# A rebuilt guess for the order of instructions, inverse roots on VectorE, and attention in smaller pieces

## The chip, the cores and the metric

The kernel runs on one core of one Trainium2 chip. The time is that of one execution on the device in microseconds; the figure for the kernel before is the median of three runs, 856.73 us (855.6 to 857.45). Engines go by the profile's names: PE is TensorE's matmuls, PEld its loads of weights, DVE is VectorE, ACT ScalarE, POOL GpSimd, and SP the queue from which the DMAs are issued.

## The reference

A trunk of two layers over 256 tokens of 2048 features. Cut to what matters:

```python
def hybrid_layer(x, c, cos, sin, layer_idx, ...):
    mod = (c @ w_ada + b_ada)[:, None, :]                  # adaLN: 2048 x 6144, one row
    shift, scale, gate = jnp.split(mod, 3, axis=-1)
    h = rms_norm(x, g_pre) * (1 + scale) + shift
    z = h @ w_in                                           # 2048 x 6144
    u, g_pool, q, k, v, g_diff = jnp.split(z, splits, axis=-1)
    pool_out = multiscale_pool(u, w_pool, pool_scale) * jax.nn.silu(g_pool)
    q, k = apply_rope(q, cos, sin), apply_rope(k, cos, sin)
    att = diff_attention(q, k, v, lam)                     # softmax(map 0) - lam * softmax(map 1), chunk-causal
    att = rms_norm(att, subln_g) * (1.0 - lam_init)        # per head of 128
    diff_out = att * jax.nn.silu(g_diff)
    y = jnp.concatenate([pool_out, diff_out], axis=-1) @ w_out   # 2048 x 2048
    return x + (1 + gate) * rms_norm(y, g_post)
```

## The kernel before

**Units.** The weights of the two projections come as tiles `raw` of 128 x 1024 float32 (512 KB). Each is split into a high and a low half that TensorE takes (`whi`, a cast on ACT; `wlo`, a subtraction on DVE), and so are the left operands (`hhi`, `hlo`). A product is hi x hi + hi x lo + lo x hi. One `raw` is one *unit* of twelve matmuls of 128 x 512 into two accumulators `acc`. A layer has 96 units of the input projection (12 blocks of 512 columns, 8 pairs of row tiles each) and 32 of the output projection. The text numbers units and raws through both layers from 0: layer 0 has 0 to 95 and 96 to 127, layer 1 128 to 223 and 224 to 255. "Slot 225" is the place in PE's order where 225 units are done. The ring of `raw` has four buffers, those of `whi` and `wlo` three, PSUM four banks for `acc` and four for the rest (`ps`).

**AdaLN.** The row `mod` is no matmul. A tile `ada` of 512 KB (ring of three) is loaded, and one DVE instruction multiplies it by the broadcast `c` and sums along the row (method `ada`): 184 such products beside eight at the start. Each column's pair of products ends with three small steps into `A` and `B`, which `make_h` needs. The last third of a layer gives its gate `G`.

**Side work.** Beside the units run generators, each a chain of pieces: `make_h` (normalized operands), `rope`, `pool_group` (trailing means as products with `band`, then `ps<-hf,Gw`, `z<-ps,cols,z` and the parts `hhi`, `hlo`), and `heads` for a pair of heads: scores (`ps<-z,z`), maxima `nm`, exponentials `t` on ACT, 1/sum `rs`, combined maps, their transposes (`ps<-consts,t`), copies `aT` on ACT, value products (`ps<-z,aT`), squares `ass`, inverse root, scaled product `z<-ps,af,z`, and `make_cat`, which transposes the result (`ps<-consts,z`) and splits it. Units of the output projection need these parts (`cat`), four of pool groups and four of pairs of heads.

**Order.** All engines run in program order (`tc.manual_schedule()`), and the program decides it while it is written. `Watched` (L70) passes each instruction to `Clock.note` (L103), which keeps a guess of each engine's time, so in the profile every instruction bears the line L86. After each unit, `advance` (L679) lets those side pieces run whose inputs are due by the guess within `SLACK` of TensorE's guessed time and for which PSUM banks are free. Then `beside` (L757) takes the `ada` products that have been dealt to the unit: while VectorE's guessed time is not ahead of TensorE's, and in any case until no more than `TODO` = 1 is left over.

**Inverse roots.** `rsqrt` (L282) serves the pre-norm of layer 0 (`xr`, two columns) and every pair of heads (`ar`, four columns): GpSimd forms x, DVE a guess from the bits of x in two steps, GpSimd three Newton rounds of four steps; `heads` then multiplies by `r2` there. `rms` (L304) does the other norms (`ya`, `yb`, `xa`, `xb`) on DVE, one column each.

## Time and profile before

| | before |
|---|---|
| median of three runs | 856.73 us |
| profiled execution | 856.63 us |
| its span | 854.8 us |
| granted clock over the span | 0.986 |
| VectorE | 899 rows of its order, 695.5 us busy (81%) |
| ScalarE | 543.5 us busy (64%) |
| GpSimd | 45.8 us busy (5%), 129 instructions |
| DMA | 245.08 MB, mean 287 GB/s |

The page's table of 40 slices shows where the layers lie: a slice is 21.4 us, a digit the busy tenths in it, and PEclk the granted clock.

```profile
PE   3899899999999999998979999999999999889995
DVE  6789898888898977988786788888789989667665
POOL 2000000000000001142000000000000000030400
PEclk9999999999999999999989999999999999999998
DMA  9899999999898975688925999999998888443742
```

Slices 15 to 18 are layer 0's attention, 20 and 21 the turn-over to layer 1, 34 to 37 layer 1's attention; POOL's digits stand where the inverse roots are.

### The profile page before, as it was taken

What the parts mean: (1) busy time and instruction counts of PE and PEld (TensorE: products, weight loads), DVE (VectorE), ACT (ScalarE), POOL (GpSimd) and SP (SyncE); (2) the same over time, 40 slices, a digit from 0 to 9 for tenths busy, and PEclk for the clock granted to TensorE, in tenths of its full rate; (3) what the DMA queues carried; (4) which work ended last, traced back from release to release, by engine and by line L of the source; (5) the groups of instructions that cost most, each with busy time, mean ns of one, the idle gap of its engine ahead of it and who ended that gap; (6) DMA issues with size and microseconds to landing.
All of it is one profiled execution on the core that took longest, in us unless ns stands there. A gap on an engine that the chain in (4) does not pass through costs nothing.

```text
span 854.8 us, 11938 instructions
## 1 busy us (share of the span) xinstructions
PE 803.6 (94%) x4058; PEld 667.5 (78%) x4058; DVE 695.5 (81%) x1194; ACT 543.5 (64%) x950; POOL 45.8 (5%) x129
## 2 busy tenths in 40 slices
PE   3899899999999999998979999999999999889995
PEld 1678688889888887786758888888889898677884
DVE  6789898888898977988786788888789989667665
ACT  4688787766556666664655656776665567666561
POOL 2000000000000001142000000000000000030400
PEclk9999999999999999999989999999999999999998
DMA  9899999999898975688925999999998888443742
GB/s 340 287 396 327 330 370 344 370 367 350 304 355 325 331 251 166 207 287 292 324 73 182 343 365 383 326 346 322 357 326 333 309 320 265 130 148 109 261 148 99
DMA packets 68239, 245.08 MB, mean 287 GB/s; under 512 B 7729, under 2 KB 8017, under 8 KB 67665
## 3 DMA queue, kind: packets, MB, share of 16 engines
q1 hardware_dynamic: 67890, 244.14, 80.3%
q8 instruction: 32, 0.52, 0.3%
q10 hardware_dynamic: 288, 0.17, 0.1%
q14 instruction: 29, 0.24, 0.1%
HBM read 242.17 MB, written 2.11 MB: 286 GB/s over the span
## 4 chain that ended last, share of the span: by engine, by line
PE 75%; DVE 10%; ACT 5%; DMA 4%; POOL 3%; issue 2%; SPq 0%; DVEq 0%; ACTq 0%
PE acc L86 69%; PE ps L86 6%; DVE wlo L86 3%; ACT whi L86 2%; POOL arh L86 2%; DVE ada L86 2%; DMA raw<-in_w_out 1%; ACT t L86 1%; DMA z<-in_w_ada 1%; DVE z L86 1%; DMA ada<-in_w_ada 1%; DVE rt L86 1%; DMA raw<-in_w_in 1%; DVE x L86 1%; ACT sqj L86 1%
## 5 line engine op out<-in xcount | busy, mean ns | idle before, releaser
L86 ACT CAST whi<-raw 128x1024 fp32r<-128x1024 f32 x247 | 259.4, 1053 | 205.1 <-PE acc L86 182.7
L86 DVE TENSOR_TENSOR wlo<-raw,whi 128x1024 fp32r<-128x1024 f32 x247 | 301.3, 1223 | 81.2 <-ACT whi L86 80.7
L86 PE MATMUL acc<-whi,hhi 128*128 128x512 f32 x860 | 344.3, 400 | 6.0 <-ACT hhi L86 2.5
L86 PE MATMUL acc<-whi,hlo 128*128 128x512 f32 x860 | 337.8, 393 | 1.3 <-DVE hlo L86 1.3
L86 PE MATMUL acc<-wlo,hhi 128*128 128x512 f32 x860 | 337.8, 393 | 0.7 <-DVE wlo L86 0.7
L86 DVE SCALAR_TENSOR_TENSOR ada<-ada,cb 128x1024 f32<-128x1024 f32 x184 | 223.7, 1219 | 5.2 <-DMA ada<-in_w_ada 4.8
L86 PEld LDWEIGHTS acc<-whi,hhi 128*128 128x128 f32 x860 | 163.0, 190 | 45.0 <-ACT acc L86 4.4
L86 PEld LDWEIGHTS acc<-whi,hlo 128*128 128x128 f32 x860 | 162.7, 189 | 37.3 <-DVE hlo L86 2.6
L86 PEld LDWEIGHTS acc<-wlo,hhi 128*128 128x128 f32 x860 | 163.1, 190 | 33.8 <-DVE wlo L86 2.1
L86 ACT ACTIVATE z<-acc 128x512 f32<-128x512 f32 x164 | 88.5, 591 | 1.5 <-PE acc L86 1.5
L86 ACT COPY acc<-z 128x512 f32<-128x512 f32 x123 | 68.7, 585 | 3.1 <-DVE rt L86 3.1
L86 PE MATMUL acc<-hhi,whi 128*128 128x256 f32 x256 | 43.1, 288 | 3.1 <-ACT whi L86 2.0
L86 ACT ACTIVATE t<-ps,nm 128x128 f32<-128x128 f32 x64 | 26.0, 420 | 30.9 <-DVE nm L86 30.9
L86 POOL TENSOR_SCALAR arx<-ass 128x4 f32<-128x4 f32 x8 | 4.1, 517 | 728.6 <-ACT sqj L86 728.3
L86 PE MATMUL acc<-hlo,whi 128*128 128x256 f32 x256 | 41.7, 286 | 0.2 <-DVE hlo L86 0.2
L86 PE MATMUL acc<-hhi,wlo 128*128 128x256 f32 x256 | 41.6, 285 | 0.0
L86 PEld LDWEIGHTS acc<-hhi,whi 128*128 128x128 f32 x256 | 36.6, 193 | 5.4 <-ACT whi L86 2.4
L86 PEld LDWEIGHTS acc<-hlo,whi 128*128 128x128 f32 x256 | 35.7, 194 | 0.4 <-DVE hlo L86 0.4
L86 PEld LDWEIGHTS acc<-hhi,wlo 128*128 128x128 f32 x256 | 35.7, 194 | 0.0
L86 PE MATMUL ps<-consts,t 128*128 128x128 f32 x112 | 17.2, 284 | 17.6 <-issue 12.4
L86 PEld LDWEIGHTS ps<-consts,t 128*128 128x128 f32 x112 | 14.0, 147 | 22.0 <-issue 14.1
L86 PE MATMUL ps<-z,z 64*128 64x128 f32 (+1 forms) x128 | 19.1, 371 | 8.3 <-ACT t L86 7.5
(144 smaller groups left out, 596.8 us busy)
## 6 DMA issues: line engine op xcount, KB each, us to landing
raw<-in_w_in SPq DMA_DIRECT2D x192, 512.0 KB, 5.7
ada<-in_w_ada SPq DMA_DIRECT2D x184, 512.0 KB, 5.7
raw<-in_w_out SPq DMA_DIRECT2D x64, 512.0 KB, 4.6
z<-in_w_ada SPq DMA_DIRECT2D x8, 512.0 KB, 11.4
x<-in_x SPq DMA_DIRECT2D x2, 1024.0 KB, 7.6
Gw<-in_w_pool SPq DMA_DIRECT2D x8, 256.0 KB, 6.4
Gw<-gate SPq DMA_DIRECT2D x2, 1024.0 KB, 4.9
out<-x SPq DMA_DIRECT2D x8, 256.0 KB, 2.7
```

What stands on the lines that cost most here:

```text
L86: return f(*args, **kw)
```

## The change

Four things are done at once.

- `Clock` is rebuilt. It knows the operation of each instruction and has costs per engine (fixed, per element, for an accumulator, and until the result is seen), a price for a change of ScalarE's table, a DMA link with its rate, regions of a tile in place of whole tiles, the rings of buffers, and a TensorE that is slow for a while after a pause.
- `TODO` = (8, 1), with a method `put_off`: up to eight `ada` products may be left over, unless they are the own layer's shift or scale, when it is one; towards a layer's end the number falls with the units that are left, to none in the last five.
- `rsqrt` runs on VectorE, from x/2, with the guess in one step and each round in three (two for one column). It yields after every step, the multiplication by `r2` joins its last round, and `rms` uses it. GpSimd has no work left.
- In `heads` the copies `aT` are a step of their own, the value products a later one, and the inverse root begins a piece later. The pre-norm is one piece at the third lead product.

The matmuls, casts and loads are the same in number and shape, and `ORDERS`, `RATE`, `EARLY` and `SLACK`, which shape the plan, are unchanged. VectorE has 976 rows in place of 899.

```diff
@@ -91,34 +92,97 @@
-    FIXED = {"tensor": 0.0, "vector": 0.07, "scalar": 0.09, "gpsimd": 0.15, "sync": 0.0}
-    EACH = {"tensor": 0.42e-3, "vector": 1.04e-3, "scalar": 0.85e-3, "gpsimd": 2.3e-3, "sync": 1.43e-3}
+    COST = {"vector": (0.07, 1.05e-3, 0.01, 0.13), "scalar": (0.085, 0.86e-3, 0.13, 0.15), "gpsimd": (0.25, 2.3e-3, 0.0, 0.15)}
+    TABLES = ((AF.Exp, 1), (AF.Silu, 2), (AF.Sin, 3))
+    MB_US, LANDING = 0.40, 1.6
+    COLD = (2.0, 3.4)
+    RINGS = {"raw": 4, "ada": 3, "whi": 3, "wlo": 3, "acc": 4}
...
-    def note(self, key, outs, ins):
+    def note(self, key, op, outs, ins, total, table):
+        size = lambda x: math.prod(x.shape[1:])
+        outs, ins = ([x for x in xs if not x.tensor.name.startswith(("in_", "out_"))] for xs in (outs, ins))
+        t = was = self.now[key]
         for x in ins:
-            t = max(t, self.wrote.get(x.tensor.name, 0.0))
+            t = max(t, self.latest(self.wrote, x))
+            if key != "tensor" and x.tensor.name.startswith(("acc", "ps")):
+                t = max(t, self.latest(self.used, x))
         for x in outs:
-            if key != "tensor":
-                t = max(t, self.used.get(x.tensor.name, 0.0))
-        t += self.FIXED[key] + n * self.EACH[key]
-        self.now[key] = t
-        done = t + (1.5 if key == "sync" else 0.15)
+            if key != "tensor" or not self.wrote.get(x.tensor.name):
+                t = max(t, self.latest(self.used, x))
+        if "dma" in op:
+            self.now[key] = t + 0.35
+            x = (outs + ins)[0]
+            self.link = max(self.link, t + 0.8) + size(x) * x.shape[0] * 4e-6 / self.MB_US
+            end, done = t, self.link + self.LANDING
+        elif key == "tensor":
+            n, dt, began = size(outs[0]), ins[-1].dtype, t
+            if op == "transpose":
+                t += 0.109
+            elif dt == F32:
+                t += max(0.109, 0.835e-3 * n) * (1 if ins[0].shape[0] == DQK else 2)
+            else:
+                t += 0.0135 + 0.4167e-3 * n if dt == F32R else 0.08
+
+            if began - was > self.COLD[0]:
+                self.cold = began + self.COLD[1]
+            t = max(t, min(self.cold, 2 * t - began))
+            end, done = t, t + 0.27
+            self.now[key] = t
+        else:
+            fixed, each, accum, after = self.COST[key]
+            if table and table[0] != self.table:
+                self.table = table[0]
+                t += 1.29
+            t += fixed + each * max(size(x) for x in outs + ins) + total * accum
+            end, done = t, t + after
+            self.now[key] = t
         for x in ins:
-            self.used[x.tensor.name] = max(self.used.get(x.tensor.name, 0.0), t)
+            self.mark(self.used, x, end)
         for x in outs:
-            self.wrote[x.tensor.name] = self.used[x.tensor.name] = done
+            self.mark(self.wrote, x, done)
+            self.mark(self.used, x, done)
         self.last = max(self.last, done)
 
...
-    def rsqrt(self, ss, n, mul, tag):
-
-        gp = self.nc.gpsimd
+    def rsqrt(self, ss, n, mul, tag, end=None):
+
+
+        v = self.nc.vector
...
-        gp.tensor_scalar(x, ss, mul, EPS, op0=ALU.mult, op1=ALU.add)
+
+        v.tensor_scalar(x, ss, 0.5 * mul, 0.5 * EPS, op0=ALU.mult, op1=ALU.add)
         yield y
-        self.guess(yi, x)
-        for _ in range(3):
-            gp.tensor_tensor(h, y, y, op=ALU.mult)
-            gp.tensor_tensor(h, h, x, op=ALU.mult)
-            gp.tensor_scalar(h, h, -0.5, 1.5, op0=ALU.mult, op1=ALU.add)
-            gp.tensor_tensor(y, y, h, op=ALU.mult)
+        v.tensor_scalar(yi, x.bitcast(I32), -0.5, 0x5F3759DF - (1 << 22) - (1 << 31), op0=ALU.mult, op1=ALU.add)
         yield y
-
-    def guess(self, yi, x):
-
-        v = self.nc.vector
-        v.tensor_scalar(yi, x.bitcast(I32), 1, None, op0=ALU.logical_shift_right)
-        v.tensor_scalar(yi, yi, -1, 0x5F3759DF, op0=ALU.mult, op1=ALU.add)
+        for i in range(3):
+            v.scalar_tensor_tensor(h, y, x, y, op0=ALU.mult, op1=ALU.mult) if n == 1 else v.tensor_tensor(h, y, y, op=ALU.mult)
+            yield y
+            if n > 1:
+                v.tensor_tensor(h, h, x, op=ALU.mult)
+                yield y
+            if i == 2 and end is not None:
+                v.tensor_tensor(y, y, end, op=ALU.mult)
+            v.scalar_tensor_tensor(y, h, 1.5, y, op0=ALU.subtract, op1=ALU.mult)
+            yield y
...
     def rms(self, parts, tag):
+        s1 = self.t(self.sp, [P, 1], tag + "s")
+        self.nc.vector.tensor_reduce(s1, parts, axis=AX.X, op=ALU.add)
+        yield s1
+        yield from self.rsqrt(s1, 1, 1.0 / D, tag)
...
     def pre_norm(self):
-        for r in self.rsqrt(s1, NST, 1.0 / D, "xr"):
-            self.xr = [r[:, st : st + 1] for st in range(NST)]
-            yield
+        (r,) = self.together(self.rsqrt(s1, NST, 1.0 / D, "xr"))
+        self.xr = [r[:, st : st + 1] for st in range(NST)]
...
-    TODO = 1
+    TODO = (8, 1)
...
             if i == 2:
-                next(norm, None)
+                self.pre_norm()
...
     def beside(self, u):
         self.advance()
         self.todo += u.extras
-        while self.todo and (self.nc.now["vector"] <= self.nc.now["tensor"] + self.AHEAD or len(self.todo) > self.TODO):
+        while self.todo and (self.nc.now["vector"] <= self.nc.now["tensor"] + self.AHEAD or len(self.todo) > self.put_off()):
             self.ada(*self.todo.pop(0))
+
+    def put_off(self):
+
+        l, nt, _ = self.todo[0]
+        left = sum(u.l == self.l for u in self.units[self.at :])
+        return min(self.TODO[l == self.l and nt < 32], left - 5)
...
         yield 0
+        while self.turned_a:
+            yield 0
+        self.turned_a = True
+        aT = [self.t(self.pp, [P, 3, P], "aT") for _ in range(2)]
+        for h in range(2):
+            nc.scalar.copy(aT[h].rearrange("p i q -> p (i q)"), bt[h][:, 0 : 3 * P])
+        self.live -= 2
+        yield 1
+        self.turned_a = False
         av = self.ps()
         for h in range(2):
-            aT = self.t(self.pp, [P, 3, P], "aT")
-            nc.scalar.copy(aT.rearrange("p i q -> p (i q)"), bt[h][:, 0 : 3 * P])
-            self.live -= 1
             hs = slice((h0 + h) * P, (h0 + h + 1) * P)
...
         yield 0
...
-        (yf,) = self.together(self.rsqrt(ss, 4, 1.0 / P, "ar"))
-        f = sm("af", 4)
-        gp.tensor_tensor(f, yf, r2[:, :, 0], op=ALU.mult)
         yield 0
-        yield 0
+
```

Where instructions move, at three places. The first is VectorE in layer 0, from the `wlo` of raw 100 on; unit 99 needs the `hlo` of the last pool group, which is the second `hlo` here. Before:

```order
L86 SCALAR_TENSOR_TENSOR ada_2921,mod_166<-ada_2921,cb_92 128x1024
L86 SCALAR_TENSOR_TENSOR ada_2949,mod_166<-ada_2949,cb_92 128x1024
L86 SCALAR_TENSOR_TENSOR z_378<-ps_3166,cols_98,z_378 128x256 x2
L86 TENSOR_TENSOR hlo_3190<-z_378,hhi_3189 128x512
L86 TENSOR_TENSOR wlo_3199<-raw_2955,whi_3198 128x1024
L86 SCALAR_TENSOR_TENSOR z_378<-ps_3193,cols_98,z_378 128x256 x2
L86 TENSOR_TENSOR hlo_3238<-z_378,hhi_3237 128x512
L86 SCALAR_TENSOR_TENSOR ada_3069,mod_166<-ada_3069,cb_92 128x1024
L86 TENSOR_TENSOR wlo_3245<-raw_3017,whi_3244 128x1024
```

After the change (`nm`, RECIPROCAL, `co` and `t` belong to one pair of heads; `co` and three rows of `t` are left out):

```order
L87 SCALAR_TENSOR_TENSOR z_377<-ps_3162,cols_98,z_377 128x256 x2
L87 TENSOR_TENSOR hlo_3180<-z_377,hhi_3179 128x512
L87 TENSOR_TENSOR wlo_3184<-raw_2948,whi_3183 128x1024
L87 SCALAR_TENSOR_TENSOR ada_2942,mod_166<-ada_2942,cb_92 128x1024
L87 SCALAR_TENSOR_TENSOR ada_3007,mod_166<-ada_3007,cb_92 128x1024
L87 SCALAR_TENSOR_TENSOR ada_3065,mod_166<-ada_3065,cb_92 128x1024
L87 TENSOR_REDUCE nm_2955<-ps_3205 128x1 x2
L87 TENSOR_REDUCE nm_2955<-ps_3206 128x1 x2
L87 RECIPROCAL rs_2957<-s_2956 128x8
...
L87 SCALAR_TENSOR_TENSOR t_3235<-t_3235,co_3245 128x256
L87 SCALAR_TENSOR_TENSOR z_377<-ps_3213,cols_98,z_377 128x256 x2
L87 TENSOR_TENSOR hlo_3254<-z_377,hhi_3253 128x512
```

The last pool group's `z` and `hlo` stood right behind raw 100's `wlo`; now three products and one pair's softmax stand between.

The second place is VectorE in layer 0's output projection, from the `wlo` of raw 119 to that of raw 123. Before:

```order
L86 TENSOR_TENSOR wlo_3947<-raw_3880,whi_3946 128x1024
L86 TENSOR_TENSOR z_3953<-raw_3886,z_3952 128x1024
L86 TENSOR_TENSOR z_3958<-acc_3522,Gw_3409 128x512
L86 TENSOR_TENSOR z_3958<-acc_3523,Gw_3409 128x512
L86 SCALAR_TENSOR_TENSOR ada_3871,mod_167<-ada_3871,cb_92 128x1024
L86 TENSOR_TENSOR wlo_3979<-raw_3908,whi_3978 128x1024
L86 TENSOR_TENSOR wlo_3997<-raw_3929,whi_3996 128x1024
L86 TENSOR_TENSOR wlo_4015<-raw_3950,whi_4014 128x1024
```

After the change:

```order
L87 TENSOR_TENSOR wlo_3896<-raw_3826,whi_3895 128x1024
L87 TENSOR_TENSOR z_3902<-raw_3832,z_3901 128x1024
L87 TENSOR_TENSOR z_3907<-acc_3497,Gw_3379 128x512
L87 TENSOR_TENSOR z_3907<-acc_3498,Gw_3379 128x512
L87 SCALAR_TENSOR_TENSOR ada_3851,mod_167<-ada_3851,cb_92 128x1024
...
L87 SCALAR_TENSOR_TENSOR ada_3890,mod_167<-ada_3890,cb_92 128x1024
L87 TENSOR_TENSOR wlo_3934<-raw_3857,whi_3933 128x1024
L87 SCALAR_TENSOR_TENSOR ada_3893,mod_167<-ada_3893,cb_92 128x1024
L87 TENSOR_TENSOR wlo_3955<-raw_3875,whi_3954 128x1024
L87 SCALAR_TENSOR_TENSOR ada_3925,mod_167<-ada_3925,cb_92 128x1024
L87 TENSOR_TENSOR wlo_3976<-raw_3899,whi_3975 128x1024
```

The one product between the raws has become four, with the rows of `A` and `B` of a column left out here.

The third is VectorE in layer 1's attention, from the `wlo` of raw 227 on; each pair of heads has `nm`, RECIPROCAL, `co` and four `t`, of which the rows at the ends are shown. Before:

```order
L86 TENSOR_TENSOR wlo_7061<-raw_6875,whi_7060 128x1024
L86 TENSOR_REDUCE nm_6952<-ps_7034 128x1 x2
L86 RECIPROCAL rs_6954<-s_6953 128x8
...
L86 SCALAR_TENSOR_TENSOR t_7079<-t_7079,co_7089 128x256
L86 TENSOR_REDUCE nm_6955<-ps_7052 128x1 x2
L86 RECIPROCAL rs_6957<-s_6956 128x8
...
L86 SCALAR_TENSOR_TENSOR t_7096<-t_7096,co_7106 128x256
L86 TENSOR_TENSOR wlo_7113<-raw_6910,whi_7112 128x1024
L86 TENSOR_TENSOR wlo_7139<-raw_6948,whi_7138 128x1024
```

After the change:

```order
L87 TENSOR_TENSOR wlo_7009<-raw_6834,whi_7008 128x1024
L87 TENSOR_TENSOR wlo_7043<-raw_6873,whi_7042 128x1024
L87 TENSOR_REDUCE nm_6916<-ps_7026 128x1 x2
L87 RECIPROCAL rs_6918<-s_6917 128x8
...
L87 SCALAR_TENSOR_TENSOR t_7061<-t_7061,co_7071 128x256
L87 TENSOR_REDUCE nm_6919<-ps_7034 128x1 x2
L87 RECIPROCAL rs_6921<-s_6920 128x8
...
L87 SCALAR_TENSOR_TENSOR t_7078<-t_7078,co_7088 128x256
L87 TENSOR_TENSOR wlo_7095<-raw_6912,whi_7094 128x1024
L87 TENSOR_TENSOR wlo_7113<-raw_6972,whi_7112 128x1024
```

The two chains stood behind raw 227's `wlo` and ahead of raw 228's; now raw 228's `wlo` stands ahead of them and raw 229's behind. On PE the scores that these chains take stood at slot 225 and stand at slot 226.

## The prediction

> **What bounds the kernel now.** I read the page's shares and its chain first, then the waits of PE, then PE's timeline at each wait.

> ```profile
> span 854.8 us, 11938 instructions
> PE 803.6 (94%) x4058; PEld 667.5 (78%) x4058; DVE 695.5 (81%) x1194; ACT 543.5 (64%) x950; POOL 45.8 (5%) x129
> PE 75%; DVE 10%; ACT 5%; DMA 4%; POOL 3%; issue 2%; SPq 0%; DVEq 0%; ACTq 0%
> ```

> TensorE is busy in 94% of the span, and three quarters of the chain are its matmuls, which the change leaves alone in number and shape. A different order can therefore only win or lose part of the 854.8 - 803.6 = 51.2 us in which PE stands still, and what the throttle takes beside that. Here is what PE waited for (us in total, times, the longest):

> ```profile
> PE ps L86 <- issue: 12.4, 1, 12.4
> PE ps L86 <- ACT t L86: 7.5, 7, 2.0
> PE ps L86 <- DVE t L86: 5.3, 1, 5.3
> PE acc L86 <- DVE hlo L86: 1.5, 2, 1.3
> ```

> The 12.4 us are the start and the 5.3 us the turn-over between the layers; both hang on chains that the change barely touches. What can move are the waits of attention: 7.5 us behind ScalarE's exponentials (`t`), and single ones behind the left operands of the output projection. PE's timeline gives them one by one (start, duration, work, idle before it and who ended that):

> ```profile
> 357.48 0.70 PE L86 MATMUL ps<-z,z 64*128 64x128 f32 x5 [1.04 <-ACT t L86]
> 365.98 0.70 PE L86 MATMUL ps<-z,z 64*128 64x128 f32 x5 [0.78 <-ACT aT L86]
> 391.61 1.10 PE L86 MATMUL ps<-consts,z 128*128 128x128 f32 x4 [1.07 <-DVE z L86]
> 399.97 0.50 PE L86 MATMUL acc<-whi,hlo 128*128 128x512 f32 x1 [1.30 <-DVE hlo L86]
> 735.27 0.48 PE L86 MATMUL ps<-z,z 64*128 64x128 f32 x2 [1.51 <-ACT t L86]
> 736.07 0.70 PE L86 MATMUL ps<-z,z 64*128 64x128 f32 x5 [0.32 <-ACT t L86]
> 737.68 0.85 PE L86 MATMUL ps<-z,z 64*128 64x128 f32 x5 [0.32 <-ACT t L86]
> 761.25 0.49 PE L86 MATMUL ps<-z,z 64*128 64x128 f32 x2 [1.99 <-ACT t L86]
> 762.06 1.65 PE L86 MATMUL ps<-z,z 64*128 64x128 f32 x6 [0.32 <-ACT t L86]
> ```

> Layer 0's attention costs 1.04 + 0.78 + 1.07 + 1.30 = 4.2 us, layer 1's 2.15 us at 735 to 738 and 2.31 us at 761 to 762. The second pair costs more than its idle time. The table of stretches (busy time of PE, PEld, DVE, ACT, POOL, then granted clock, DMA share, GB/s) has:

> ```profile
> 340.00:400.00 60.00, 55.63 (x293) 44.51 (x292) 51.77 (x114) 35.62 (x92) 19.45 (x49) 1.00 0.73 252
> 400.00:430.00 30.00, 29.47 (x127) 23.56 (x128) 23.59 (x30) 17.99 (x28) 0.00 (x0) 1.00 0.91 320
> 733.00:742.00 9.00, 6.85 (x32) 4.64 (x31) 3.80 (x11) 7.10 (x26) 0.00 (x0) 0.81 0.39 117
> 760.00:770.00 10.00, 8.43 (x34) 6.52 (x35) 5.27 (x13) 5.42 (x18) 3.32 (x12) 0.83 0.18 52
> ```

> After the two waits of layer 1 the clock dropped: 9.00 x 0.19 and 10.00 x 0.17 are 1.7 us each. Layer 1's waits thus cost 2.15 + 1.7 + 2.31 + 1.7 = 7.9 us. This is the largest prize in reach.

> **The inverse root on VectorE.** Before, GpSimd did 13 small steps for a pair of heads, with two of VectorE's in between:

> ```profile
> L86 POOL TENSOR_TENSOR arh<-ary 128x4 f32<-128x4 f32 x24 | 11.2, 466 | 7.3 <-DVE ary L86 6.0
> DVE ary L86 <- POOL arx L86: 8.3, 4, 3.7
> 433.43 0.16 DVE L86 SCALAR_TENSOR_TENSOR yay<-yah,yay 128x1 f32<-128x1 f32 x1
> 433.62 0.22 DVE L86 SCALAR_TENSOR_TENSOR yah<-yay,yau 128x1 f32<-128x1 f32 x1
> 391.20 1.12 DVE L86 SCALAR_TENSOR_TENSOR z<-ps,af,z 128x128 f32<-128x128 f32 x4 [1.76 <-POOL af L86]
> 21.55 0.62 DVE L86 TENSOR_SCALAR t<-x,xry 128x256 f32<-128x256 f32 x2 [2.01 <-POOL xry L86]
> ```

> VectorE now issues 12 such steps for a pair where it issued 2. Its dependent small steps start 433.62 - 433.43 = 0.19 us apart, so a pair costs it 10 x 0.19 = 1.9 us more, the eight pairs 15 us. In exchange VectorE no longer stands 8.3 us before the guess or 1.76 us before the scaled product. In layer 0 the four chains add 7.6 us to 340 to 400, where VectorE has 60.00 - 51.77 = 8.2 us idle: it fits, though only just. The ends are -3.7 us (its longest wait for GpSimd, were all of that PE's) and +7.6 us (were none covered); I take nothing for the chain itself and let its delay count where the order below puts it on PE's path. The pre-norm's wait of 2.01 us turns into 11 dependent steps of about 0.19 us: 2.1 us of VectorE in its place, so 0 at the start (ends -0.5 and +0.5). The turn-over's and the last norm's chains lose two steps each, 0.4 us in three chains of layer 0's turn-over together and 0.2 us at the end.

> **Layer 0, unit 99.** This is the first place where the new order bears on PE. Unit 99 multiplies by the last pool group's parts, whose `z` and `hlo` stand on VectorE now behind three adaLN products (`ada`) and one pair's maxima and softmax steps.

> ```profile
> 335.42 1.22 DVE L86 SCALAR_TENSOR_TENSOR ada<-ada,cb 128x1024 f32<-128x1024 f32 x1
> 336.56 1.22 DVE L86 TENSOR_TENSOR wlo<-raw,whi 128x1024 fp32r<-128x1024 f32 x1
> 739.73 1.14 DVE L86 TENSOR_REDUCE nm<-ps 128x1 f32<-128x128 f32 x4
> 748.29 2.35 DVE L86 TENSOR_TENSOR wlo<-raw,whi 128x1024 fp32r<-128x1024 f32 x2
> 333.20 0.87 DVE L86 SCALAR_TENSOR_TENSOR z<-ps,cols,z 128x256 f32<-128x256 f32 x2
> 334.81 0.69 DVE L86 TENSOR_TENSOR hlo<-z,hhi 128x512 fp32r<-128x512 f32 x1 [0.74 <-ACT hhi L86]
> 334.25 1.50 PE L86 MATMUL ps<-z,aT 128*128 128x128 f32 x12
> ```

> ```profile
> 722.00 0.39 PE L86 MATMUL acc<-wlo,hhi 128*128 128x512 f32 x1
> 722.23 0.39 PE L86 MATMUL acc<-whi,hlo 128*128 128x512 f32 x1
> ```

> A unit is twelve matmuls that start 0.23 us apart, about 2.73 us. A product occupies VectorE for 336.56 - 335.42 = 1.14 us; maxima, exponentials and softmax steps take (748.29 - 739.73) / 2 = 4.28 us. Unit 100's `wlo` goes ahead of them and ends, by my walk along the new order, at about 332.7. Then 332.7 + 3 x 1.14 + 4.28 = 340.4, the two `z` 0.87, and ScalarE's `hhi` about 0.7: 342.0. PE came to this slot at 334.25 and has its small products to do there; one score product, the pool's product and the value products are in the slot now, which brings it to about 338.0. It waits 4.0 us. As 2.15 us in three pieces dropped the clock at 735, I charge 1.7 us too. In exchange the 4.2 us of before's four waits find their inputs ready, because VectorE does while PE stands what it did in them. Sum: 4.0 + 1.7 - 4.2 = **+1.5 us** (ends: -4.2 if the group is on time, +5.7 if no later wait goes).

> [...]

> **Layer 0's output projection.** Now up to eight products may be put off, and they come due before the layer ends. By the order, seven of them are still owed at the `wlo` of raw 119 and one at that of raw 127.

> ```profile
> 399.84 1.21 DVE L86 TENSOR_TENSOR wlo<-raw,whi 128x1024 fp32r<-128x1024 f32 x1
> 424.72 1.23 DVE L86 TENSOR_TENSOR wlo<-raw,whi 128x1024 fp32r<-128x1024 f32 x1 [2.57 <-ACT whi L86]
> ```

> That is 6 x 1.14 = 6.8 us more for VectorE, against 30.00 - 23.59 = 6.4 us idle in 400 to 430: +0.4 us if all its idle time served, +3.0 us if the last 2.57 us come too late. I take +1.0, and -0.4 for the shorter norms: **+0.6 us**. The cover is thin: each product more would cost PE its 1.14 us.

> **Layer 1's attention.** The second pair's scores go one unit later (slot 226, not 225), when ScalarE has freed their banks, so of the 2.15 + 1.7 us some 0.6 stay. But VectorE's two chains of 4.28 us now stand ahead of raw 229's `wlo`. They begin after raw 228's, near 740.9, and end at 749.5; the `wlo` is there at 750.7. PE ends unit 224 at 733.8 (735.27 - 1.51), does unit 225 by 736.5, scores and 0.6 us of waiting by 738.5, units 226 to 228 by 746.7 and a group of transposes by 747.2; so it waits 3.4 us for unit 229, with 1.7 us of clock behind it. The wait at 761 goes whole. With 1.5 us more for the last pairs' operands (a walk along the order, ends 0 and 3.5) the stage loses 0.6 + 3.4 + 1.7 + 1.5 = 7.2 us against 7.9: **-0.7 us** (ends -5.8 if 229 is on time, +1.3).

> **The rest.** In early layer 0 some pieces change places around units 10 to 20. PE's waits there are among these:

> ```profile
> PE acc L86 <- ACT acc L86: 2.4, 2, 1.9
> PE acc L86 <- ACT z L86: 1.2, 1, 1.2
> ```

> By the order the 1.2 us grow somewhat and the 1.9 us shrink: +0.3 us (ends -1 and +1), an estimate. In layer 1 the late products have slack by my walk: the last of them ends near 800 and the gate is used after 815. The other pieces hide behind matmuls. Sum: 0 + 0.3 + 1.5 + 0.6 - 0.7 - 0.2 = +1.5 us on the profiled execution's 856.63 us, which stands 0.1 us below the median of 856.73: **858.1 us**. About 0.2%, 1.7 us, is what a measurement of this kernel tells from no change, so "same" is 855.0 to 858.4.

> **The rivals.** *The waits go and nothing takes their place* (0.30). VectorE idles 8.2 us in 340 to 400, and ScalarE more; if the softmax steps run ahead of my walk by a unit (2.7 us), units 99 and 229 wait 1 us or so without the clock. Then layer 1 gives -5.1 in place of -0.7, layer 0 about -1 in place of +1.5: 858.1 - 4.4 - 2.5 = 851.2, and 853 where one of the two holds; I write 852 (850 to 855). Against it: both chains are strictly serial on VectorE in the order's rows.

> *The products put off saturate the output projection of layer 0* (0.20). DMA stands at a share of 0.91 in 400 to 430 at 320 GB/s. A raw or `ada` tile is 512 KB:

> ```profile
> ada<-in_w_ada SPq DMA_DIRECT2D x184, 512.0 KB, 5.7
> ```

> Between raws 119 and 131 twelve raws and eleven `ada` tiles of 0.52 MB fall due where it was four: 12 MB in 12 x 2.73 = 33 us, 365 GB/s, against 320 / 0.91 = 352 at a full share. That is 1.2 us late by bandwidth alone; if VectorE also has no cover, the group before the turn-over starts 1.2 + 3.0 + 1.0 us later than I charged: 863 us (861 to 865). It decides from the point where more than five products are owed at raw 119; the order says seven. Against it: DMA had slack before 400, and raws fetched early there lighten the rest.

> *The order turns out not to matter* (0.08): PE's waits shift but keep their sum, as ring depths and not program order set them; 856.6.

> **How the numbers follow.** The forecast has 0.42 and by itself a range of 855.5 to 861; half of it lies within 0.2%, half slower. Faster: 0.30 + 0.01 = 0.31. Same: 0.21 + 0.06 = 0.27. Slower: 0.21 + 0.20 + 0.01 = 0.42. A tenth is left out below 851, in the first rival, and somewhat under a tenth above 863.5.

> **What would show it.** Right: POOL's busy time near zero and VectorE's up by some 14 us; no PE wait at 735 to 738 and at 761; one of 3 to 5 us before a product with the fourth pool group's `hhi` near 340, with the clock down behind it; one of 3 us behind `wlo` near 748; waits of 0.5 to 1 us behind `wlo` at 412 to 425, DMA share there above 0.95. Wrong: if those at 340 and 748 are missing the first rival holds; if the turn-over begins 5 us later than 430, the second.

## The result, and the profile after

| | before | after |
|---|---|---|
| median (lowest to highest) | 856.78 us (855.6 to 857.45) | 870.02 us (868.26 to 870.63) |
| ratio, 95% interval | 1 | 1.0153 (1.0134 to 1.0171) |
| profiled execution, its span | 856.63 us, 854.8 us | 870.22 us, 868.4 us |

Two executions among the experiments below, one of 1626 us (b3) and one of 1349 us (e2), are left out of their medians and ratios.

The changed kernel is 1.5% slower. The forecast of 858.1 us said slower by about a tenth of this, and the range, up to 863.5 us, missed it too. The head of the page after, with the shares of the chain and the rows of the 40 slices for VectorE, GpSimd and the granted clock:

```profile
span 868.4 us, 11915 instructions
PE 808.9 (93%) x4058; PEld 671.6 (77%) x4058; DVE 708.4 (82%) x1271; ACT 543.5 (63%) x950; POOL 0.2 (0%) x4
DVE  7788899888888966789986788788888979667765
POOL 0000000000000000000000000000000000000000
PEclk9999999999999998999979999999999999999998
PE 68%; DVE 16%; DMA 6%; ACT 5%; issue 4%; SPq 0%; DVEq 0%; ACTq 0%
```

GpSimd is empty and VectorE has 12.9 us more, as forecast. PE's idle time grew from 51.2 to 868.4 - 808.9 = 59.5 us, and its busy time by 5.3 us with the same matmuls. Of that 868.4 x 0.019 - 854.8 x 0.014 = 4.5 us is clock, which fell from 0.986 to 0.981 over the span. In the chain 7% of the span went from PE to VectorE (10% to 16%) and DMA (4% to 6%). What PE waited for after the change (us in total, times, longest):

```profile
PE acc L87 <- ACT hhi L87: 6.6, 6, 2.5
PE acc L87 <- DVE wlo L87: 5.1, 4, 2.4
PE acc L87 <- ACT acc L87: 3.3, 5, 1.0
PE ps L87 <- ACT t L87: 3.1, 3, 2.1
PE acc L87 <- DVE hlo L87: 2.1, 1, 2.1
```

The waits behind the exponentials `t` fell from 7.5 to 3.1 us, which the change was able to do; in their place PE waits for operands of the big products, `hhi`, `wlo` and `hlo` (3.1, 0.7 and 1.5 us before). PE's timeline after, at the waits that the text uses:

```profile
344.51 0.59 PE L87 MATMUL acc<-whi,hhi 128*128 128x512 f32 x1 [2.45 <-ACT hhi L87]
416.81 0.80 PE L87 MATMUL acc<-wlo,hhi 128*128 128x512 f32 x1 [2.37 <-DVE wlo L87]
759.19 0.49 PE L87 MATMUL acc<-whi,hhi 128*128 128x512 f32 x1 [1.14 <-ACT whi L87]
761.33 0.79 PE L87 MATMUL acc<-wlo,hhi 128*128 128x512 f32 x1 [1.65 <-DVE wlo L87]
800.37 1.60 PE L87 MATMUL ps<-z,aT 128*128 128x128 f32 x12 [1.01 <-DVE hlo L87]
815.39 1.01 PE L87 MATMUL ps<-consts,z 128*128 128x128 f32 x4 [0.53 <-DVE z L87]
819.00 0.63 PE L87 MATMUL acc<-whi,hlo 128*128 128x512 f32 x1 [2.12 <-DVE hlo L87]
```

To see where the 13.6 us of span arise, the two traces are laid beside each other by units: for each unit the start of its first matmul after, less that before. The growth of this difference over a stretch of units is what the stretch lost.

| units | lost | forecast |
|---|---|---|
| start to 95 | +0.7 | +0.3 |
| 95 to 116 (layer 0's attention) | +2.8 | +1.5 |
| 116 to 127 (layer 0's output projection) | +4.5 | +1.0 |
| 127 to 219 (turn-over, layer 1's input projection) | +1.0 | -0.4 |
| 219 to 238 (layer 1's attention) | -1.9 | -2.2 |
| 238 to 243 (last operands) | +6.7 | +1.5 |
| 243 to the end | -0.2 | -0.2 |

Two rows hold most of the miss: 3.5 us in layer 0's output projection and 5.2 us at layer 1's last operands. Of the second, about 1.3 us is a group of value products (804.57 to 805.82) that stood ahead of unit 238 before and changed rows; units 219 to 243 together lost 4.8 us, where the forecast had -0.7. The first, as stretches of whole units (116 to 125; busy time of PE, PEld, DVE, ACT, POOL, then clock, DMA share, GB/s). Before:

```profile
402.38:428.12 25.74, 25.21 (x110) 20.04 (x108) 19.33 (x25) 16.14 (x24) 0.00 (x0) 1.00 0.94 332
```

After:

```profile
405.90:436.20 30.30, 26.84 (x110) 21.12 (x109) 28.90 (x46) 15.45 (x23) 0.00 (x0) 0.94 0.97 351
```

VectorE went from 19.33 to 28.90 us: eleven products where there were three, 8 x 1.14 = 9.1 us. It stood idle for 6.4 us of the stretch before; after, it is busy in 95% of it. Of PE's 4.6 us more, 2.9 are idle time and 1.6 are busy time at the lower clock (0.94) that follows the wait of 2.37 us. DMA is nearly full as well (a share of 0.97).

### The profile page after: what moved, and what is told of

Read it like the earlier page. It is cut to its first block, busy times and chain, and to the rows that moved or that the text cites. A ratio compares the mean times of both kernels' runs of the same rounds, so it can differ in the third digit from the quotient of the medians.

```text
span 868.4 us, 11915 instructions
## 1 busy us (share of the span) xinstructions
PE 808.9 (93%) x4058; PEld 671.6 (77%) x4058; DVE 708.4 (82%) x1271; ACT 543.5 (63%) x950; POOL 0.2 (0%) x4
## 4 chain that ended last, share of the span: by engine, by line
PE 68%; DVE 16%; DMA 6%; ACT 5%; issue 4%; SPq 0%; DVEq 0%; ACTq 0%
PE acc L87 63%; DVE wlo L87 5%; PE ps L87 5%; DMA ada<-in_w_ada 4%; DVE ada L87 3%; DVE z L87 2%; ACT whi L87 2%; DMA raw<-in_w_in 1%; DMA z<-in_w_ada 1%; DVE rt L87 1%; ACT t L87 1%; DVE t L87 1%; ACT z L87 1%; ACT hhi L87 1%; DVE arh L87 0%
## 5 line engine op out<-in xcount | busy, mean ns | idle before, releaser
L87 DVE TENSOR_TENSOR wlo<-raw,whi 128x1024 fp32r<-128x1024 f32 x247 | 300.2, 1222 | 81.7 <-ACT whi L87 81.0
L87 PE MATMUL acc<-whi,hhi 128*128 128x512 f32 x860 | 346.2, 403 | 12.4 <-ACT hhi L87 6.0
L87 PE MATMUL acc<-z,hhi 128*128 128x512 f32 x72 | 22.3, 391 | 0.6 <-ACT acc L87 0.6
L87 DVE TENSOR_TENSOR hlo<-hf,hhi 128x512 fp32r<-128x512 f32 (+1 forms) x15 | 9.8, 656 | 14.3 <-ACT hhi L87 13.1
## 6 DMA issues: line engine op xcount, KB each, us to landing
raw<-in_w_in SPq DMA_DIRECT2D x192, 512.0 KB, 5.6
ada<-in_w_ada SPq DMA_DIRECT2D x184, 512.0 KB, 6.0
raw<-in_w_out SPq DMA_DIRECT2D x64, 512.0 KB, 4.3
z<-in_w_ada SPq DMA_DIRECT2D x8, 512.0 KB, 11.4
```

Of the source, the lines that this page charges most:

```text
L87: return f(*args, **kw)
```

## The experiments

Each run is set beside the kernel before on the same chip; the ratio carries the 95% interval, and two runs are compared by their ratios, since they can come from different chips. The columns on the right are the loss by stretches of units as above, from the one profiled execution of each run. Single executions scatter: b3 and e2, which have the same order up to unit 95, begin it 3 us apart. So a row's first column and its sum are good to some 3 us, a stretch further on to about 1.

| run | median us | ratio (95%) | to 116 | 116-127 | 127-219 | 219-243 |
|---|---|---|---|---|---|---|
| the change | 870.0 | 1.0153 (1.0134-1.0171) | +3.5 | +4.5 | +1.0 | +4.8 |
| a5_no_debt | 871.3 | 1.0171 (1.0143-1.0199) | +13.6 | -0.5 | -0.3 | +4.8 |
| a3_old_clock | 859.8 | 1.0054 (1.0035-1.0073) | +7.2 | -1.3 | -0.6 | -3.1 |
| a2_gp_roots | 867.5 | 1.0135 (1.0114-1.0155) | +8.0 | -1.2 | -0.5 | +3.4 |
| a4_before_roots | 861.9 | 1.0070 (1.0045-1.0094) | +8.8 | -1.2 | -0.2 | -0.9 |
| b3_roots_same_order | 860.5 | 1.0050 (1.0030-1.0069) | +1.0 | -0.5 | -0.2 | +1.5 |
| b1_clock_only | 863.6 | 1.0074 (1.0045-1.0102) | +4.0 | -1.2 | +1.5 | +3.8 |
| b2_pieces | 867.7 | 1.0123 (1.0107-1.0138) | +12.4 | -1.2 | +0.2 | -0.5 |
| b4_roots_double | 876.7 | 1.0226 (1.0210-1.0243) | +11.6 | -0.4 | -0.2 | +7.1 |
| g1_one_round | 862.1 | 1.0045 (1.0028-1.0061) | +3.8 | +3.4 | +0.1 | -1.9 |
| a6_hold99 | 872.5 | 1.0181 (1.0156-1.0206) | +8.1 | +4.0 | +0.7 | +4.5 |
| c4_pool98 | 872.3 | 1.0183 (1.0159-1.0207) | +9.0 | +2.2 | +0.6 | +4.6 |
| c1_slack4 | 887.5 | 1.0364 (1.0331-1.0396) | +10.9 | +4.7 | +7.1 | +6.1 |
| c3_tail | 871.7 | 1.0172 (1.0155-1.0189) | +2.8 | +4.9 | +0.2 | +4.0 |
| f3_price_line | 866.7 | 1.0103 (1.0085-1.0122) | +4.7 | -1.2 | -0.7 | +5.2 |
| f1_cheap_again | 879.3 | 1.0262 (1.0212-1.0311) | +18.8 | +0.9 | +2.1 | +1.4 |
| g2_half_products | 864.8 | 1.0088 (1.0064-1.0112) | +4.3 | +2.2 | +0.3 | +4.9 |
| e1_before_held6 | 859.5 | 1.0034 (1.0019-1.0049) | -3.6 | +4.5 | +0.4 | 0.0 |
| e2_b3_held6 | 864.6 | 1.0081 (1.0050-1.0112) | +0.7 | +6.7 | -0.1 | +1.2 |

### Taking parts of the change back

**a5_no_debt**: from unit 103 to the end of layer 0 only one product may be left over.

```diff
-        return min(self.TODO[l == self.l and nt < 32], left - 5)
+        return min(1 if 103 <= self.at < 128 else self.TODO[l == self.l and nt < 32], left - 5)
```

> The change, but from unit 103 to the end of layer 0 only one adaLN product may be left over (before: 1, the change: up to 8), so the debt of eight products never builds up; on PE only two groups of transposes move by a unit. If the debt costs what the unit times show (PE falls from +3.5 us at unit 119 to +8.0 us at unit 125), it gives back 4 to 5 us: 865 to 866 us, no wait for wlo near 417 and no half clock behind it. If the loss there is only the late attention pushed on (rival), it gives back less than 1 us: 869 to 870.

The loss of units 116 to 127 goes (+4.5 to -0.5), so the products that are left over make it. But 10 us appear ahead of it, where the products now stand in attention; PE's waits between 340 and 418 us of this run begin with

```profile
PE acc L87 <- DVE hlo L87: 3.7, 1, 3.7
PE acc L87 <- ACT hhi L87: 2.5, 1, 2.5
PE ps L87 <- ACT aT L87: 2.4, 1, 2.4
```

Two groups of transposes stand one unit later here as well (slots 111 and 114 in place of 110 and 113). With the change's guess, leaving products over is not a loss on balance. Layer 1 does not move.

**a3_old_clock**: the change, with the `Clock` and `Watched` of before and `TODO = (1, 1)`; roots and pieces of the change stay.

> The change with the guess of before (Clock and Watched as before, TODO 1); the inverse roots stay on VectorE and attention stays in the smaller pieces. If the order that the rebuilt guess lays out is the cause, it comes back to the time before or under it: 853 to 857 us. If the roots on VectorE or the smaller pieces are the cause (rival), it stays at 862 us or more, with VectorE's waits on PE's path in attention.

Two thirds of the loss go, 1.0153 to 1.0054, and layer 1 (219 to 243) is 3.1 us better than before instead of 4.8 us worse. The time lies between the two that were expected. What the new guess orders, with the products that it leaves over, is the larger part of the loss.

**a2_gp_roots**: the change, with `rsqrt` on GpSimd as before.

> The change with the inverse roots back on GpSimd as before (rsqrt, guess and rms as before), rebuilt guess, debt of eight and the smaller pieces kept. If the order is the cause it stays slow, 867 to 872 us. If the roots on VectorE cost (rival), it gives back 3 us or more: 866 or less.

It gains 0.2%, not enough to tell from the change by these intervals, and layer 1's loss stays. The roots on VectorE alone are not the cause.

### Parts of the change alone, in the kernel before

**b3_roots_same_order**: pairs' roots on VectorE as twelve steps in one go, while the guess is told GpSimd's old steps, so that every other instruction keeps its place.

```diff
-        (yf,) = self.together(self.rsqrt(ss, 4, 1.0 / P, "ar"))
-        f = sm("af", 4)
-        gp.tensor_tensor(f, yf, r2[:, :, 0], op=ALU.mult)
+        f = self.rsqrt_v(ss, 1.0 / P, "ar", r2[:, :, 0])
```

> The kernel before with the eight chains of attention's inverse root on VectorE at the very places in program order where GpSimd had them (the guess still books them on GpSimd, so no instruction of PE, ACT or SP moves; the pre-norm stays on GpSimd). If VectorE has no cover for 12 dependent steps a pair, layer 0's attention is 5 to 8 us late at unit 116 as in the kernel with the roots alone (+8.8), total 860 to 864 us. If the loss of that kernel came from the order that its guess chose (rival), it is within 2 us of before: 854 to 858.

It costs 0.5%. VectorE's timeline in this run shows how:

```profile
354.63 0.15 DVE L313 TENSOR_SCALAR arx<-ass 128x4 f32<-128x4 f32 x1
...
356.67 0.16 DVE L320 SCALAR_TENSOR_TENSOR arf<-arh,ary 128x4 f32<-128x4 f32 x1
356.75 1.14 DVE L86 TENSOR_REDUCE nm<-ps 128x1 f32<-128x128 f32 x4
```

and PE's:

```profile
358.42 0.70 PE L86 MATMUL ps<-z,z 64*128 64x128 f32 x5 [2.89 <-ACT t L86]
```

The chain of 356.75 - 354.63 = 2.1 us stands ahead of another pair's maxima `nm`. Their exponentials, and the scores that need the banks, come later: before, PE waited 1.04 us at this place, here 2.89 us. Behind this wait PE's matmuls of 128x512 start 0.43 us apart from 359.87 to 362.85 and 0.23 us apart after that: a clock of about half (0.23 / 0.43). Before, it stayed whole here (1.00 over 357 to 366). Of the 3.6 us that units 95 to 116 lose in this run 2.0 are PE's idle time and 1.6 its busy time, which is this clock. That VectorE has idle time elsewhere in the stage does not help.

**a4_before_roots**: the same, but the old guess sees the steps and orders by them.

> The kernel before with only the inverse roots moved to VectorE (old guess, old pieces of attention). If the roots are free or a small gain: 853 to 857.5 us, with VectorE's 8.3 us of waiting for GpSimd gone and 15 us more busy time. If 12 dependent steps of 0.19 us a pair sit on PE's path (rival): 859 us or more.

0.7%; seeing them did not help the order.

**b2_pieces**: only attention's separate pieces, with GpSimd's roots and the old guess.

> The kernel before with attention's copies and value products as separate pieces, and nothing else of the change (guess of before, roots on GpSimd). From the two kernels that differ by these pieces (859.75 and 861.9) they give 2 us: 853.5 to 855.5. If they gave that only with roots on VectorE (rival): 856 to 860.

This alone costs 1.2%, all of it by unit 116. In its order the transposes of the four pairs' results stand in layer 0 at slots 105, 108, 112 and 115 where they stood at 103, 108, 112 and 113: a piece more in each chain, and the last pair is late. The time lies above both that were expected. With roots on VectorE the same pieces cost nothing that can be seen (a4 to a3, 1.0070 to 1.0054). The parts do not add up.

**b1_clock_only**: only the new `Clock` and `Watched`.

> The kernel before with the rebuilt guess alone (roots on GpSimd, attention's pieces and one product left over as before). If the guess alone costs, by pieces that it takes later: 861 to 868 us, with layer 1 between units 219 and 243 3 us or more behind before. If it costs only together with the finer pieces (rival): 855 to 859.

0.7%, with layer 1's loss of +3.8 us in it. So that loss comes with the guess, without roots, pieces or `TODO`.

### How much VectorE's chain costs

**b4_roots_double**: b3 with six Newton rounds for three. The six leave the factor with the other sign, so attention's part of the output is reversed, other than its expectation says.

```diff
-        for i in range(3):
+        for i in range(6):
```

> The kernel with the roots on VectorE in before's very order, with six Newton rounds in place of three (the result is the same): nine steps more a pair, 9 x 0.195 = 1.8 us, 14 us of VectorE in all. If VectorE's steps sit on PE's path, another 3 to 7 us: 863 to 868. If the loss there was something else (the order of semaphores, chance), it stays at 859 to 862.

**g1_one_round**: the change's very order, with one round in `ar` (a coarser root), the guess being told all three.

```diff
+            if tag == "ar" and i < 2:
...
+                continue
```

> The change in its very order, with one Newton round in place of three in attention's inverse roots (less exact; six steps of 0.195 us less a pair, 1.2 us, 9.4 us of VectorE in all; the guess books them as before). If VectorE's time is on PE's path, 5 to 9 us less: 861 to 865. If PE waits for other things, 868 to 870.

By the ratios, nine steps more for each of eight pairs cost 15 us over b3, and six steps less gain 9 us on the change. By the 0.19 us from one step to the next in the traces that is 14 us and 9 us of VectorE: in total, all of it is PE's time. Place by place it is not so even. In g1 the 24 steps less of layer 0 gain 0.3 us between units 95 and 116 and 1.1 us up to 127. The gain lies in layer 1: with the same order 219 to 243 takes 97.9 us instead of 104.6. That stretch after the change:

```profile
718.41:822.97 104.56, 96.06 (x497) 76.81 (x498) 79.03 (x187) 63.18 (x159) 0.00 (x0) 0.97 0.55 176
```

and with one round:

```profile
716.71:814.60 97.89, 93.51 (x499) 75.64 (x498) 74.65 (x162) 63.18 (x159) 0.00 (x0) 0.98 0.55 176
```

VectorE is idle for 25 us in the first of these, and yet 4.4 us less of its work gain 6.7 us. The wait of 2.12 us at 819.00 has become this one:

```profile
812.20 0.50 PE L87 MATMUL acc<-whi,hlo 128*128 128x512 f32 x1 [0.88 <-DVE hlo L87]
```

The clock stays whole behind this shorter wait (the matmuls start 0.23 us apart from 812.53 on); after the change it is 0.55 over 819.60 to 823.00, and that is 1.7 of the 6.7 us.

VectorE's timeline after the change, ahead of 819.00, shows the chain that it ends:

```profile
812.65 0.16 DVE L87 TENSOR_SCALAR arx<-ass 128x4 f32<-128x4 f32 x1
...
814.70 0.16 DVE L87 SCALAR_TENSOR_TENSOR ary<-arh,ary 128x4 f32<-128x4 f32 x1
814.89 1.13 DVE L87 SCALAR_TENSOR_TENSOR z<-ps,ary,z 128x128 f32<-128x128 f32 x4
815.93 1.22 DVE L87 TENSOR_TENSOR wlo<-raw,whi 128x1024 fp32r<-128x1024 f32 x1
817.07 1.22 DVE L87 TENSOR_TENSOR z<-raw,z 128x1024 fp32r<-128x1024 f32 x1
818.20 0.74 DVE L87 SCALAR_TENSOR_TENSOR hlo<-ps,cols,hhi 128x512 fp32r<-128x512 f32 x1
```

Root, scaled product, two subtractions for the weights, `hlo`. ScalarE's `hhi`, the last input, is done at 817.13, but `hlo` waits behind the subtractions until 818.20. From 803.52 to here VectorE has no pause, so every step ahead of `hlo` moves it, and PE's units behind it.

### Removing single waits

**a6_hold99**: the change without products at unit 99 (`self.at != 99` in `beside`). **c4_pool98**: `SLACK` 3 at unit 98 alone, which puts the last pool group's product back to slot 98.

> The change without the three adaLN products that it puts on VectorE before the last pool group's parts (they follow a unit later). If they are what unit 99 waits for, its start falls from +7.9 us behind before to +4.5 or less and the half clock near 345 goes; by the end 2 to 5 us are left of it: 865 to 868 us. If VectorE's whole load in layer 0's attention decides (rival), the lead is gone again by unit 116 and the time stays at 869 to 871.

> The change with SLACK 3.0 at unit 98 alone: the last pool group's product goes to slot 98, where it was before, ahead of the next pair's scores, so its parts no longer stand behind that pair's softmax steps on VectorE. If this place is what unit 99 waits for, its start falls from +7.9 us behind before to +3 or less. What is left of it at unit 116 tells whether the stall of unit 99 costs anything in the end: 5 us of it if PE is the bound there (total 864 to 866), none if VectorE's chain of pieces is (868 to 872).

Neither gains. c4 does remove the wait that the prediction saw: unit 99 begins 0.7 us after that of before instead of 7.9. But by unit 116 it is 9.0 us behind instead of 3.5, and its waits between 340 and 418 us now begin with

```profile
PE acc L87 <- DVE hlo L87: 2.9, 1, 2.9
PE ps L87 <- ACT t L87: 2.8, 2, 1.8
```

The prediction held that VectorE catches up while PE stands at unit 99, so that without the stall the arrears are paid later. This run agrees but does not show it, for the rest of the order did not stay: the transposes of the pairs' results stand at slots 104, 108, 112 and 115 where the change has 102, 107, 110 and 113 (in a6 103, 107, 110 and 114). Where VectorE's arrears go in the change's own order is not shown.

**c1_slack4**: `SLACK` 4 everywhere, so that pieces run earlier. **c3_tail**: 2.5 from unit 227 on, which puts layer 1's last pieces about a unit earlier.

> The change with SLACK 4.0 in place of 1.0, so that a piece may be taken up to 4 us before its inputs are due by the guess. On PE, layer 1's last transposes of attention come at slots 236, 237, 238, 239 in place of 236, 238, 241, 242. If pieces taken too late are the cause, the stalls at units 238 to 243 of layer 1 go (4 to 6 us) and layer 0 gains too: 860 to 865 us. If early pieces only move PE's waits to their own inputs (rival): 868 us or more.

> The change with SLACK 2.5 from unit 227 of layer 1 on (1.0 before that): on PE every later piece of layer 1's attention comes exactly one unit earlier (transposes of the results at slots 235, 237, 240, 241 in place of 236, 238, 241, 242), and nothing else moves. In all kernels with the rebuilt guess so far, units 238 to 243 took 21 to 24 us, with the guess of before 14.6 to 14.9. If that is one unit of lateness in the chain of pieces, the stretch falls to 15 to 18 us and the total to 863 to 867. If it only moves the wait forward to units 228 to 238 (rival, as SLACK 4.0 everywhere did): the total stays at 868 to 872.

"The pieces run too late" was a theory of mine, and it falls: everywhere it costs 2% more, and in the tail alone it gains nothing: units 238 to 243 take 19.6 us instead of 21.25, but the value products that left the stretch account for 1.3 us of that, the waits in it grow from 2.65 to 3.60 us, and the time is the same.

### One line of the guess

**f3_price_line**: the kernel before with one line of the new `Watched`.

```diff
             if "out" not in kw:
-                outs.append(aps.pop(0))
+                outs.insert(0, aps.pop(0))
```

> The kernel before with one line of Watched as in the change: the tile comes ahead of accum_out among an instruction's outputs. The old guess prices an instruction by its first output, so an adaLN product cost it 0.07 us (one element) where the trace has 1.14 us a product; with the line it is priced at 1.13. If this line makes the order that costs, the kernel comes to that of the rebuilt guess alone: 861 to 867 us, units 238 to 243 of layer 1 take 20 us or more (before 14.6). If other parts of the rebuilt guess do (regions, latencies, tables, rings), it stays at 855 to 859.

It prices an instruction by its first output. An `ada` product has a sum as second output; the old line put that first, so the old guess took a product for one element, 0.07 us; with the new line it is 1024 elements, 1.14 us, which is what the trace shows. The same line prices anew the other instructions that sum along a row, exponentials and some squares; the run does not part them from the products. These truer prices cost 1.0%, with +5.2 us in layer 1. In its order the maps' transposes of layer 1 stand at slots 230, 231, 238 and 239 (before 227, 228, 235, 236), and the last two pairs' results at 242 and 243 (240, 242). A guess whose engines have more to do lets the side pieces run later, and the last ones have few units left behind them. Two of PE's waits grew in this run, from 1.1 and 0.7 us before:

```profile
PE ps L86 <- DVE z L86: 3.4, 2, 2.3
PE acc L86 <- DVE wlo L86: 3.0, 2, 1.8
```

One of each lies in layer 1, 1.17 us at 809.29 and 1.20 us at 752.34.

**f1_cheap_again**: the change with every instruction that sums along its row (products, exponentials, squares) priced as one element.

```diff
-            t += fixed + each * max(size(x) for x in outs + ins) + total * accum
+            t += fixed + each * (1 if total else max(size(x) for x in outs + ins)) + total * accum
```

> The change, with instructions that sum along the row priced as before by one element (products, exponentials, squares), all else of the rebuilt guess kept. If the price is the cause, 860 to 864 us, near the change with the whole old guess (859.75), units 238 to 243 of layer 1 at 15 to 17 us. If other parts of the guess decide: 867 us or more.

Layer 1's loss falls from +4.8 to +1.4 us, so these prices do make it there too. Layer 0 loses 15 us more by unit 116, though only 12 products stand between units 97 and 116 where the change has 9, and VectorE is idle there for 26.5 us in place of 17.1; part of it waits for the products' loads (7.1 us). Why the order is so poor there is open. The old price by itself does not bring the old order back.

### Products held back, by themselves

**g2_half_products**: the change's order, with layer 1's products of layer 0 over half their row (layer 1's shift and scale are then others).

> The change in its very order, with layer 1's adaLN products that run in layer 0 computed over half their row (layer 1's shift and scale are wrong; the loads are the same). Each takes 0.53 us less, some 9 us of VectorE between units 103 and 127. If VectorE sets the loss in layer 0's output projection, units 116 to 125 fall from 30.2 to 26 us and the total to 864 to 866. If the DMA does (share 1.01 at 397 GB/s in 420 to 430 of the change), the stretch keeps 29 us or more and the total 868 to 870.

With half the VectorE time the loss in 116 to 127 is half (+4.5 to +2.2). Of that gain 1.1 us is PE's busy time (25.74 us in units 116 to 125 in place of 26.84), for the clock stays whole there (1.00). The other half of the loss is with DMA, whose share is 1.02 at 397 GB/s over 405 to 436, or with other work; that split is not settled further.

**e1_before_held6** and **e2_b3_held6**: the order of PE and ScalarE of before, and of b3; on VectorE up to six of layer 1's products are held back from slot 102 to 116 and done one a unit from 117 on. The loads of later products, which need their buffers, come later with them.

> The kernel before in its very order of TensorE and ScalarE, GpSimd's roots kept; only on VectorE up to six of layer 1's products that stand in slots 102 to 116 of layer 0 are held back, and done from slot 117 on, one a unit. Debt theory (from the run without products left over, where units 116 to 125 took 25.2 us instead of 30.2 but units 97 to 116 took 90.0 instead of 80.1): in an order that isn't otherwise worse, six products of 1.14 us less on VectorE in units 102 to 116 take away part of the four waits there (4.2 us) and cost less than that behind, because VectorE has 6.4 us idle in units 116 to 125 there: 853.5 to 856. Rival (in the old order VectorE isn't what units 102 to 116 wait for, GpSimd's and ScalarE's chain is): the same within 1 us, or 1 to 3 us slower where units 116 to 125 become as full as in the change (30.2 us).

> The same holding back in the run of the old order with roots on VectorE (860.6 us). If VectorE's chain is what PE waits for in units 97 to 116 (theory), six products less there give back most of the 5 us that the roots cost in units 99 to 112, and 1 to 3 us are lost again at units 116 to 125: 856 to 859. Rival (the roots cost where they stand in the chain, and products aren't in their way): 860 to 863.

e1 is the price of what the prediction charged with 1.0 us, by itself; it does not part VectorE's work from the loads that go with it. The stretch of units 116 to 125 in it:

```profile
398.80:429.10 30.30, 26.12 (x110) 19.96 (x109) 26.72 (x42) 15.96 (x24) 0.00 (x0) 1.00 0.99 358
```

It takes the same 30.3 us as after the change, against 25.7 before. PE waits 2.6 us behind `wlo` and 1.6 us behind ScalarE's `acc`. Two of the four waits behind `wlo`:

```profile
408.42 0.50 PE L86 MATMUL acc<-wlo,hhi 128*128 128x512 f32 x1 [1.08 <-DVE wlo L86]
414.72 0.50 PE L86 MATMUL acc<-wlo,hhi 128*128 128x512 f32 x1 [0.57 <-DVE wlo L86]
```

Holding back shortens units 97 to 116 from 78.1 to 75.1 us, as the theory had it, and costs 4.5 us behind. In medians it is 0.34% slower. My theory, that it would win by itself, falls. In e2's trace it is the same: units 97 to 116 take 78.1 us in place of b3's 81.7, and the projection loses 7 us more. None of the 18 runs beat the kernel before.

## Why the prediction was wrong

**Right in kind.** GpSimd went to 0.2 us and VectorE gained 12.9 us (forecast 14). The waits of layer 1 behind `t` went. Unit 99 waits for `hhi` (2.45 us, forecast 4.0), with the clock near half behind it (0.56). Unit 229's wait, forecast as 3.4 us behind `wlo` near 748, stands as 1.14 + 1.65 us at 759 and 761, when the 9 us that the kernel is behind by then are taken off. The stretch 219 to 238, where these sit, gave -1.9 us (forecast -2.2), though 1.3 us of that only moved behind unit 238. Waits behind `wlo` and a DMA share above 0.95 in layer 0's projection came, but one wait was 2.37 us where I had 0.5 to 1, and unit 127 begins 8.0 us later than before; a turn-over 5 us late was the second rival's sign.

**Layer 0's output projection, the first term that failed.** "I take +1.0" was mis-sized: it measured 4.5 us (and 4.5 in e1, where only six products and the loads behind them move). I counted six products where eight came, and trusted that VectorE's 6.4 us of idle time would cover them. 9.6 us of work went into a cover of 6.4, of which 5.0 were used: 4.6 are left over. In PE's terms 2.9 of them are idle time and 1.6 the lower clock behind a wait of 2.37 us, a term that I had put at nothing here. My upper end was 3.0. How much of it VectorE sets and how much DMA is open (g2). The second rival, at 863 us, told this stage nearly right; it needed the rest of the forecast to hold.

**Layer 1's last operands, the second.** "1.5 us more for the last pairs' operands (a walk along the order, ends 0 and 3.5)" measured 6.7 us. The walk put the pieces into their slots, but let the twelve steps of the root be free: "I take nothing for the chain itself". g1 shows that they are not: with the order kept, 9 us of steps are worth about 9 us, 6.7 of them in layer 1. In PE's terms the row of the last operands holds 2.65 us of waits (0.53 and 2.12), 1.7 us of half clock behind the second, which I had not charged here either, and the 1.3 us that changed rows. VectorE is not the cause by itself: a2, with the roots on GpSimd under the new guess, takes 24.5 us for units 238 to 243, more than the change's 21.25. It is the late place of the pieces, and then the length of what stands ahead of `hlo`. And I read the order without asking why the guess had moved these pieces late; f3 shows that one line about prices does that, and my list of what the new `Clock` knows didn't have it.

**The roots' cover, a step behind the second but not the first.** "It fits, though only just": 7.6 us into 8.2 us of idle time. VectorE's idle time there lies in single waits (before: 3.9 us for `t`, 3.3 us for GpSimd's roots, 1.0 us for `whi`), while the chain stands in front of particular rows. In b3, where only the roots are moved, it costs 0.5%, and 1.85 us of it at one wait (2.89 against 1.04) and 1.6 us in the half clock behind it. Layer 0's output projection loses as much with GpSimd's roots (e1).

**Layer 0's attention** was sized at +1.5 and came to +2.8. Its give-back was right: between units 99 and 116 the kernel made good 4.4 of 7.9 us (forecast 4.2). Whether the wait could be taken out at a gain is open: c4 took it out and lost more behind it, in an order that was otherwise later too.

**The first rival** (0.30, the waits go and nothing takes their place) fell: the waits went, and others came. That the turn-over gains by shorter norms (-0.4) fell too; the stretch up to unit 219 lost 1.0 us, and no run tells why.

**How the parts share the loss.** Roots and pieces together are +0.5% (a3). The new guess, with the products it leaves over, brings it to +1.5%. Taken singly in the kernel before, roots (a4), pieces (b2) and guess (b1) cost 0.7, 1.2 and 0.7%, more than all together, so no division of the 13.6 us by parts is exact. Why the truer guess makes the poorer order beyond the price of the products is open: its rules (`SLACK`, `AHEAD`, the plan) were the same, and c1 and c3 tried only one of them.

## What to carry to other kernels

Idle time of an engine over a stage is no cover for work that must stand at one place in its order, as b3 (0.5%) and g1 (9 us) show: ask which row the new steps stand ahead of, and which engine waits for that row. When work is put off, price it where it falls due, at the full length of each piece, once the idle time there is used up. And a truer cost model is a different order, which can be a slower one (f3, 1.0%): rules that were set against a wrong price may have to be set again, which no run here tried in full.

## What the hardware showed that was not expected

Behind waits like these PE's clock drops for stretches of one length. After the change it is 0.50 for 3.41 us from each of 324.29, 344.77, 416.45, 761.20 and 819.22, and at the turn-over for 10.24 us, three times as long. Two windows of 3.40 us that take in most of such a stretch (columns as above):

```profile
345.20:348.60 3.40, 3.40 (x10) 2.70 (x10) 3.16 (x6) 2.92 (x16) 0.00 (x0) 0.56 0.24 46
324.70:328.10 3.40, 3.40 (x13) 2.97 (x13) 3.38 (x9) 1.12 (x4) 0.00 (x0) 0.56 0.08 10
```

The second follows this wait:

```profile
323.20 0.70 PE L87 MATMUL ps<-z,z 64*128 64x128 f32 x5 [2.09 <-ACT t L87]
```

Before, the same place had a wait of almost the same length, and the clock stayed whole:

```profile
322.41 0.70 PE L86 MATMUL ps<-z,z 64*128 64x128 f32 x5 [2.00 <-ACT t L86]
```

```profile
320.00:328.00 8.00, 6.00 (x35) 4.89 (x36) 6.49 (x17) 4.37 (x17) 0.00 (x0) 1.00 0.27 75
```

A step of 128x4 on GpSimd lasted mostly 0.2 us but at times 1.25 us (shortest, median, longest in ns, from the groups of the tile `arh` before):

```profile
L86 POOL TENSOR_TENSOR arh<-ary x24: 197/198/1251, 338.3 to 801.3; 128x4 f32<-128x4 f32 x24
```

On VectorE after the change all 24 such steps took 161 to 164 ns. Before, each of the 17 steps of the pairs' roots that took over 0.7 us began during a `wlo` or an `ada` product of VectorE, 1.22 us long, and ended 0.05 to 0.06 us after it.
